# The delta output's gating in two parts: scaling two chunks ahead and transposing one chunk ahead of the product, in one raw tile each, with the first two chunks scaled in the attention half

## The chip, the cores and the metric

The kernel runs on one core of one Trainium2 chip. The metric is device time in microseconds (us), the median of the runs; lower is better. The engines are TensorE (PE, matmuls and transposes; PEld is its weight load), VectorE (DVE), ScalarE (ACT), GpSimd (POOL), and SyncE (SP), which here only issues DMAs. Each takes its instructions in the order of its own queue.

## The reference

One encoder layer in float32 over 1024 tokens of width 1024: a windowed attention (8 heads of 64) and a gated delta rule in both directions (4 heads of 128) read the same projection. Their outputs stand side by side and go through one output matrix. Then comes a feed-forward part (FFN) of width 4096.

```python
xn = _rmsnorm(h, norm_mix_w[l])
proj = xn @ w_in[l]
...
o_fwd = _chunk_gated_delta_rule(q, k, v, g[:, :, 0], beta[:, :, 0])
o_bwd = flip(_chunk_gated_delta_rule(flip(q), flip(k), flip(v), flip(g[:, :, 1]), flip(beta[:, :, 1])))
o = _rmsnorm(o_fwd + o_bwd, norm_w) * jax.nn.silu(z.astype(f32).reshape(B, S, GDN_HEADS, GDN_HEAD_DIM))
...
h = h + jnp.concatenate([attn, gdn], axis=-1) @ w_out[l]
hn = _rmsnorm(h, norm_ffn_w[l])
h = h + jnp.square(jax.nn.relu(hn @ w_ffn_in[l])) @ w_ffn_out[l]
```

The lines that matter here are `o`, the "delta output": per token and head it is divided by its root mean square, multiplied by a weight and by the gate silu(z), and multiplied with the lower half of `w_out`.

## The kernel before

Tokens are worked on in eight chunks of 128, numbered 7 down to 0 in the output stage. Each float32 product is made of three products of rounded parts: every operand is split into a high part (a cast on ACT, `split`, L123) and a low part (the difference, POOL, L124). `mm3` (L136 to L138) issues high by high, high by low, low by high.

The stage around the change is two streams woven together by `weave`. One is the output: `attention`, then `out_attn` (the attention half of the output product, chunks 7 to 0, two halves of 12 matmuls each with the output's columns), then `columns` (the operands of the first FFN column group, from the first FFN weights), then `out_all` (the delta half). The other is the delta rule's two scans. `scan` (L789) goes over the chunks one after the other; each step is a chain of small PE products (L820) and DVE steps (L833, L838, L839, L848, L859, L866). The backward scan goes from chunk 7 to 0, adds its part to the output `o` of the chunk (L866), and enters the chunk in `self.scanned`.

`out_gdn` (L915) prepares one chunk of the delta half:

- the load of silu(z) from DRAM to `zc[:, 0]` (SP, L919);
- four squares with their sums (ACT, L924), four small steps (DVE, L926 to L929), a power (POOL, L930);
- the scaling of `o` into `zc[:, 1]` (DVE, L931);
- four transposes (PE, L935), held behind the last product issued by `issue_after(self.summing)`;
- the gating by weight and silu(z) into `mix` (DVE, L936);
- cast and split into `mh` and `ml` (ACT L123, POOL L124), the operands of the chunk's product.

`out_all` (L941) calls it for up to three chunks in advance while they are scanned, and then issues the product (`out_gemm`, L892). That adds each half to the chunk's row `h` (DVE, L900). The row is stored (L953) and normalised for the FFN (ACT L213, POOL L200 and L201, DVE L215). From the fifth chunk on, the transposes of normalised rows for the FFN (`tokens_second`, PE L219) are woven in.

Buffers come from pools of fixed number by tag. Raw tiles (`wr`) have 4 buffers: the attention half's loaded rows, the first FFN weights (two, held until late in the stage), and `mix` and `zc` of each delta chunk. `pt` has 12, PSUM has 4 for `psA` and 4 for `psB`. A load waits on SP until its buffer is free, and SP's queue waits with it.

The order on each engine is not the order of the code: a scheduler fixes it when the program is built, from its own estimate of times, with the code's order as priority. So a change of the code may also exchange instructions elsewhere.

Of the kernel before, what the change touches and what calls it, by code (L numbers as in the profile page):

```python
# [17 lines left out]
P = 128  # L18
SEQ = 1024
D = 1024  # L20
NT = SEQ // P
NK = D // P
HALF = 512
GH = 4
# [54 lines left out]
class Block:  # L79
# [823 lines left out]
    def out_attn(self):  # L903

        while len(self.wo[0]) < 4:
            yield 0.5
        for c in range(NT - 1, -1, -1):
            mix = self.wr((P, 4, P))
            self.nc.sync.dma_start(out=mix, in_=self.mad[c].rearrange("p (g q) -> p g q", g=4))
            mh, ml = self.pt((P, 4, P), F32R), self.pt((P, 4, P), F32R)  # L910
            self.split(mix, mh, ml)
            self.h[c] = self.load_x(c)
            yield from self.out_gemm(self.h[c], mh, ml, self.wo[0])

    def out_gdn(self, c):  # L915

        nc = self.nc
        mix, zc = self.wr((P, GH, P)), self.wr((P, 2, GH, P))
        nc.sync.dma_start(out=zc[:, 0], in_=self.zd[:, :, c * P:(c + 1) * P].rearrange("h p t -> p h t"))  # L919
        o = self.o[c // 2][:, c % 2]  # L920
        so, f = self.small((P, GH)), self.small((P, GH))
        scr = self.small((P, P), bufs=2, tag="scr")
        for h in range(GH):
            nc.scalar.activation(out=scr, in_=o[:, h, :], func=AF.Square, accum_out=so[:, h:h + 1])  # L924
        s2 = self.sq2[:, :, c]
        nc.vector.tensor_tensor(out=so, in0=so, in1=s2, op=ALU.mult)  # L926
        nc.vector.tensor_scalar(out=so, in0=so, scalar1=1.0 / P, scalar2=EPS, op0=ALU.mult, op1=ALU.add)
        nc.vector.reciprocal(out=so, in_=so)
        nc.vector.tensor_tensor(out=so, in0=so, in1=s2, op=ALU.mult)  # L929
        nc.gpsimd.tensor_tensor(out=f, in0=so, in1=self.half_exp[:, 0:4], op=ALU.pow)  # L930
        nc.vector.tensor_tensor(out=zc[:, 1], in0=o, in1=f.unsqueeze(2).to_broadcast([P, GH, P]), op=ALU.mult)  # L931
        ps = self.ps("psA", (P, GH, P))
        with self.tc.issue_after(self.summing):
            for h in range(GH):
                nc.tensor.transpose(ps[:, h, :], zc[:, 1, h, :], self.ident)  # L935
        nc.vector.scalar_tensor_tensor(out=mix, in0=ps, scalar=self.w_gdn, in1=zc[:, 0], op0=ALU.mult, op1=ALU.mult)  # L936
        mh, ml = self.pt((P, GH, P), F32R), self.pt((P, GH, P), F32R)
        self.split(mix, mh, ml)
        return mh, ml

    def out_all(self, chunks):  # L941
        while len(self.wo[1]) < 4:
            yield 0.5
        ready, coming = [], list(chunks)
        for c in chunks:
            while c not in self.scanned:
                yield 0.5
            while coming and coming[0] in self.scanned and len(ready) < (3 if coming[0] else 2):
                ready.append(self.out_gdn(coming.pop(0)))
            if self.summed:  # L950
                self.norm_h(self.summed[-1])
            yield from self.out_gemm(self.h[c], *ready.pop(0), self.wo[1])
            self.nc.sync.dma_start(out=self.hd[c], in_=self.h[c])  # L953
            self.summed.append(c)

# [340 lines left out]
    def phases(self):  # L1296
# [11 lines left out]
        for half in range(2):  # L1308
# [5 lines left out]
            else:  # L1314
# [12 lines left out]
        self.kc, self.qc = [None] * 4, [None] * 4  # L1327
        self.qs = []
        self.wo, self.hnt, self.scanned, self.summed, self.rows = [{}, {}], [None, None], set(), [], {}
        run(weave((chain(self.proj_conv(C_GV, "v"), self.proj_z(), self.proj_attn()), 145.0),  # L1330
                  (chain(self.prep(), self.eliminate(), self.diag_blocks(), self.invert(tt, (0, 1))), 100.0)))
        self.bias_table()
# [91 lines left out]
```

## Time and profile before

| what | value |
|---|---|
| median of 3 runs | 1226.01 us (1224.49 to 1228.44) |
| the profiled execution | 1226.09 us |
| its span in the profile | 1224.0 us |
| mean granted PE clock | 0.989 |
| PE busy from 450 to 500 us | 49.64 of 50 us |
| PE busy from 500 to 550 us | 47.21 of 50 us |
| PE busy from 550 to 600 us | 46.48 of 50 us |
| PE busy from 600 to 650 us | 47.17 of 50 us |
| PE busy from 700 to 800 us | 99.97 of 100 us |

A row of the timeline gives the start, the duration, the engine, the source line, the operation, output and inputs by name, and in brackets the idle time before it with what ended it. A row of a line's or tile's view gives the count and the shortest, median and longest duration in ns. A row of the table of stretches gives the length and then the busy time of each engine with the count of its instructions; PEclk is the clock that PE was granted, as a share of full speed. Matmuls overlap: one of 128x512 shows about 390 ns, but the next starts 0.23 us later. The attention half of the output product lies at about 457 to 513 us, the delta half at about 513 to 588.

### The profile page before, as it was taken

The numbers are of one execution on the slowest core, as the hardware profiler recorded it, in microseconds if no ns is written. First come the engines' busy times: TensorE is split into PE (matmuls) and PEld (weight loads), VectorE is DVE, ScalarE is ACT, GpSimd is POOL, SyncE is SP. The second block draws the span as 40 slices with busy tenths as digits, with TensorE's granted clock in tenths as the row PEclk, the third lists the DMA queues.
The fourth block names the chain that finished last, engine by engine and source line by source line (L and its number), as shares of the span: only waits on it lengthen the run. The fifth ranks groups of instructions, "written<-read, shape, count | busy, mean of one in ns | idle before, by whom it ended". The sixth has DMA issues, their size and how long they took to land. (4 is left out here: it accounts for less than half of the span.)

```text
span 1224.0 us, 18445 instructions
## 1 busy us (share of the span) xinstructions
PE 1173.7 (96%) x6482; PEld 961.9 (79%) x6482; DVE 855.7 (70%) x1482; ACT 610.4 (50%) x1331; POOL 560.2 (46%) x470
## 2 busy tenths in 40 slices
PE   6999999899889999998999999999999999999997
PEld 5788878687768878887788888888878888888885
DVE  4676667993489996675855454453698796987976
ACT  6455688425376662124755454554555444344443
POOL 5354312224321233232764453635456565565695
PEclk9999999899989999999999999999999999999999
DMA  6134344433645577222144444344789534343323
GB/s 244 52 103 145 92 170 152 162 123 113 207 146 182 157 249 269 76 95 100 56 154 157 146 154 164 130 155 146 240 275 317 200 103 163 131 159 116 103 86 138
DMA packets 121629, 187.62 MB, mean 153 GB/s; under 512 B 11043, under 2 KB 64416, under 8 KB 121537
## 3 DMA queue, kind: packets, MB, share of 16 engines
q1 hardware_dynamic: 103876, 155.20, 38.4%
q10 hardware_dynamic: 17661, 31.24, 6.8%
q8 instruction: 51, 0.84, 0.3%
q14 instruction: 41, 0.34, 0.1%
HBM read 122.39 MB, written 63.49 MB: 152 GB/s over the span
## 5 line engine op out<-in xcount | busy, mean ns | idle before, releaser
L136 PE MATMUL psA<-pg,wh 128*128 128x512 f32 x416 | 165.0, 397 | 2.1 <-ACT pt L473 2.1
L138 PE MATMUL psA<-pg,wl 128*128 128x512 f32 x416 | 164.5, 395 | 0.0
L137 PE MATMUL psA<-pg,wh 128*128 128x512 f32 x416 | 164.2, 395 | 0.0
L124 POOL TENSOR_TENSOR wl<-wr,wh 128x512 fp32r<-128x512 f32 x44 | 66.8, 1540 | 156.5 <-ACT wh L123 128.7
L1194 DVE TENSOR_TENSOR pg<-pg 128x512 fp32r<-128x512 f32 x112 | 124.3, 1145 | 12.9 <-ACT pg L1193 12.9
L124 POOL TENSOR_TENSOR wh<-wr,wh 128x512 fp32r<-128x512 f32 x32 | 47.0, 1487 | 138.2 <-ACT wh L123 138.2
L1111 ACT ACTIVATE pt<-pt 128x512 f32<-128x512 f32 x64 | 40.3, 632 | 122.6 <-DVE pt L1101 122.6
L136 PE MATMUL psA<-pg,pg 128*128 128x512 f32 x256 | 98.7, 391 | 0.9 <-DVE pg L1239 0.9
L137 PE MATMUL psA<-pg,pg 128*128 128x512 f32 x256 | 99.2, 391 | 0.1
L138 PE MATMUL psA<-pg,pg 128*128 128x512 f32 x256 | 99.2, 389 | 0.0
L136 PEld LDWEIGHTS psA<-pg,wh 128*128 128x128 f32 x416 | 78.8, 190 | 19.5 <-ACT pt L473 2.4
L137 PEld LDWEIGHTS psA<-pg,wh 128*128 128x128 f32 x416 | 78.7, 189 | 17.9 <-issue 0.9
L138 PEld LDWEIGHTS psA<-pg,wl 128*128 128x128 f32 x416 | 78.7, 189 | 16.7
L124 POOL TENSOR_TENSOR pg<-wr,pg 128x512 fp32r<-128x512 f32 x48 | 73.2, 1559 | 37.9 <-ACT pg L123 37.9
L1193 ACT CAST pg<-pg 128x512 fp32r<-128x512 f32 x112 | 66.7, 620 | 36.4 <-DMA pg<-sd 31.3
L137 PE MATMUL psB<-pg,pg 128*128 128x512 f32 x192 | 74.9, 390 | 0.8 <-POOL pg L124 0.7
L136 PE MATMUL psB<-pg,pg 128*128 128x512 f32 x192 | 74.7, 389 | 0.0
L138 PE MATMUL psB<-pg,pg 128*128 128x512 f32 x192 | 74.7, 389 | 0.0
L123 ACT CAST wh<-wr 128x512 fp32r<-128x512 f32 x76 | 43.6, 623 | 52.1 <-PE psA L137 31.9
L1101 DVE TENSOR_TENSOR pt<-psB,pt 128x512 f32<-128x512 f32 x39 | 26.9, 690 | 57.6 <-PE psB L138 40.7
L1101 DVE TENSOR_TENSOR pt<-psA,pt 128x512 f32<-128x512 f32 x39 | 26.7, 689 | 51.3 <-PE psA L138 34.1
L136 PEld LDWEIGHTS psA<-pg,pg 128*128 128x128 f32 x256 | 48.0, 188 | 12.1 <-DVE pg L1239 2.1
(395 smaller groups left out, 3234.8 us busy)
## 6 DMA issues: line engine op xcount, KB each, us to landing
sd<-pt ACTq DMA_DIRECT2D x112, 256.0 KB, 2.1
pg<-sd SPq DMA_DIRECT2D x112, 256.0 KB, 2.9
wr<-in_w_ffn_in SPq DMA_DIRECT2D x32, 512.0 KB, 3.6
wr<-in_w_in SPq DMA_DIRECT2D x22, 512.0 KB, 4.2
pg<-in_x SPq DMA_DIRECT2D x16, 512.0 KB, 5.0
wr<-in_w_ffn_out SPq DMA_DIRECT2D x16, 512.0 KB, 4.7
sc<-kvd SPq DMA_DIRECT2D x14, 512.0 KB, 3.7
kvd<-pt SPq DMA_DIRECT2D x16, 256.0 KB, 2.4
```

The lines of the kernel that those rows point to most:

```text
L123: a = nc.scalar.copy(out=h, in_=raw)
L124: b = (eng or nc.gpsimd).tensor_tensor(out=l, in0=raw, in1=h.bitcast(F32), op=ALU.subtract)
L136: nc.tensor.matmul(ps, wh, xh, start=first, stop=False, skip_group_check=onto)
L137: nc.tensor.matmul(ps, wh, xl, start=False, stop=False, skip_group_check=onto)
L138: return nc.tensor.matmul(ps, wl, xh, start=False, stop=last, skip_group_check=onto)
L1101: self.nc.vector.tensor_tensor(out=out, in0=in0, in1=in1, op=ALU.add)
L1111: self.nc.scalar.activation(out=c, in_=c, func=AF.Relu)
L1193: nc.scalar.copy(out=s[:, 0], in_=raw)
L1194: v.tensor_tensor(out=s[:, 1], in0=raw, in1=s[:, 0].bitcast(F32), op=ALU.subtract)
```

## The change

`out_gdn` is cut into two. `out_scaled` does everything up to the scaling and returns the chunk and its raw tile. `out_gated` does the transposes, the gating and the split. The gated result is written over the scaled tile `zc[:, 1]`, and the tile `mix` is gone.

In the attention half, chunk 7 is scaled after attention chunk 2's product, chunk 7 is gated after chunk 1's, and chunk 6 is scaled after chunk 0's. In the delta half, before the product of chunk c, all chunks down to c−2 are scaled (waiting, in the generator, for the scan to have passed them) and all down to c−1 are gated.

```diff
             yield from self.out_gemm(self.h[c], mh, ml, self.wo[0])
-
-    def out_gdn(self, c):
-
-        nc = self.nc
-        mix, zc = self.wr((P, GH, P)), self.wr((P, 2, GH, P))
+            if c in (2, 0):
+                while self.coming[0] not in self.scanned:
+                    yield 0.5
+                self.scaled.append(self.out_scaled(self.coming.pop(0)))
+            if c == 1:
+                self.ready.append(self.out_gated(*self.scaled.pop(0)))
+
+    def out_scaled(self, c):
+
+        nc = self.nc
+        zc = self.wr((P, 2, GH, P))
...
         nc.vector.tensor_tensor(out=zc[:, 1], in0=o, in1=f.unsqueeze(2).to_broadcast([P, GH, P]), op=ALU.mult)
+        return c, zc
+
+    def out_gated(self, c, zc):
+
+        nc = self.nc
+        mix = zc[:, 1]
         ps = self.ps("psA", (P, GH, P))
...
-        ready, coming = [], list(chunks)
         for c in chunks:
-            while c not in self.scanned:
-                yield 0.5
-            while coming and coming[0] in self.scanned and len(ready) < (3 if coming[0] else 2):
-                ready.append(self.out_gdn(coming.pop(0)))
+            while self.coming and c - self.coming[0] < 3:
+                while self.coming[0] not in self.scanned:
+                    yield 0.5
+                self.scaled.append(self.out_scaled(self.coming.pop(0)))
+            while self.scaled and c - self.scaled[0][0] < 2:
+                self.ready.append(self.out_gated(*self.scaled.pop(0)))
...
-            yield from self.out_gemm(self.h[c], *ready.pop(0), self.wo[1])
+            yield from self.out_gemm(self.h[c], *self.ready.pop(0), self.wo[1])
```

In the changed kernel the lines are numbered anew: the load of z is L925, the squares L930, the small steps L932 to L935, the power L936, the scaling L937, the transposes L947, the gating L948, and the first FFN sums L1086 and L1088 (before L1073 and L1075).

Three places show how the queues change. The first is PE's queue where the attention half ends. Before, `psA_5527` is attention chunk 0's product, and `psA_5578` and `psA_5604` are the transposes of delta chunks 7 and 6; the `psB` rows are scan products.

```order
L138 MATMUL psA_5527<-wh_4792,pt_5508 128x512
L935 MATMUL psA_5578<-ident,wr_5563 128x128 x4
L820 MATMUL psB_5227<-sc_5066,pg_3943 128x128 x2
L820 MATMUL psB_5232<-sc_5162,pt_5164 128x128 x2
L820 MATMUL psB_5255<-sc_5162,pg_3942 128x128 x2
L820 MATMUL psB_5260<-sc_5162,pg_3942 128x128 x2
L935 MATMUL psA_5604<-ident,wr_5589 128x128 x4
L820 MATMUL psB_5265<-sc_5250,pg_2578 128x128 x2
```

In the changed kernel `psA_5506` is attention chunk 1's product, `psA_5520` the transposes of delta chunk 7, and `psA_5538` and `psA_5552` the two halves of attention chunk 0's product.

```order
L138 MATMUL psA_5506<-wh_4792,pt_5469 128x512
L947 MATMUL psA_5520<-ident,wr_5451 128x128 x4
L820 MATMUL psB_5208<-sc_5162,sc_5161 128x128 x2
L820 MATMUL psB_5213<-sc_5162,sc_5161 128x128 x2
L820 MATMUL psB_5218<-sc_5066,pg_3943 128x128 x2
L820 MATMUL psB_5223<-sc_5162,pt_5164 128x128 x2
L820 MATMUL psB_5227<-sc_5066,pg_3943 128x128 x2
L820 MATMUL psB_5232<-sc_5162,pt_5164 128x128 x2
L136 MATMUL psA_5538<-pg_4677,pt_5532 128x512
L137 MATMUL psA_5538<-pg_4678,pt_5532 128x512
L136 MATMUL psA_5552<-pg_4677,pt_5532 128x512
L137 MATMUL psA_5552<-pg_4678,pt_5532 128x512
```

Chunk 7's transposes moved ahead of attention chunk 0's product, and that product now stands between scan products.

The second place is PE's queue at delta chunk 1's transposes. Before, `psA_5840` is chunk 4's product, `psA_5871` are chunk 1's transposes, and `psA_5888` is chunk 3's product; no scan product is left.

```order
L138 MATMUL psA_5840<-pg_4971,pt_5691 128x512
L935 MATMUL psA_5871<-ident,wr_5856 128x128 x4
L136 MATMUL psA_5888<-pg_5155,pt_5753 128x512
L137 MATMUL psA_5888<-pg_5156,pt_5753 128x512
L138 MATMUL psA_5888<-pg_5155,pt_5754 128x512
```

In the changed kernel `psA_5885` is chunk 3's product, `psA_5915` are chunk 1's transposes, and `psA_5933` is chunk 2's product.

```order
L820 MATMUL psB_5493<-sc_5429,pt_5431 128x128 x2
L820 MATMUL psB_5497<-sc_5340,pg_3716 128x128 x2
L820 MATMUL psB_5502<-sc_5429,pt_5431 128x128 x2
L137 MATMUL psA_5885<-pg_4971,pt_5799 128x512
L138 MATMUL psA_5885<-pg_4970,pt_5800 128x512
L947 MATMUL psA_5915<-ident,wr_5839 128x128 x4
L136 MATMUL psA_5933<-pg_5155,pt_5860 128x512
L137 MATMUL psA_5933<-pg_5156,pt_5860 128x512
```

Chunk 1's transposes moved one product later, and the scan's last products now lie within chunk 3's product.

The third place is DVE's queue at the first FFN sums, which read both first FFN weight tiles. Before, they stand where attention chunk 3's additions (`pg_5281`) are.

```order
L900 TENSOR_TENSOR pg_5281<-pg_5281,psA_5325 128x512
L1073 SCALAR_TENSOR_TENSOR pt_5545<-wr_5541,wr_5543 128x512
L848 SCALAR_TENSOR_TENSOR sc_5066<-sc_4977,egl,psB_5112 128x128 x2
L1075 TENSOR_TENSOR wr_5541<-wr_5541 128x4x128
L848 SCALAR_TENSOR_TENSOR sc_5066<-sc_4977,egl,psB_5117 128x128 x2
```

In the changed kernel `pg_5536` is attention chunk 0's row, and `wr_5602` is delta chunk 5's raw tile.

```order
L833 SCALAR_TENSOR_TENSOR sc_5250<-psB_5255,negc,sc_5250 128x128 x2
L937 TENSOR_TENSOR wr_5602<-dbl_4251,sm_5605 128x512
L833 SCALAR_TENSOR_TENSOR sc_5250<-psB_5260,negc,sc_5250 128x128 x2
L1086 SCALAR_TENSOR_TENSOR pt_5585<-wr_5581,wr_5583 128x512
L1088 TENSOR_TENSOR wr_5581<-wr_5581 128x4x128
L900 TENSOR_TENSOR pg_5536<-pg_5536,psA_5538 128x512
L838 TENSOR_TENSOR sc_5251<-psB_5265,w_533 128x256
L839 TENSOR_TENSOR sc_5251<-psB_5265,cc 128x256
```

The sums moved three chunks later, between two steps of the scan. On SP the load of the second weight tile (L254) now stands behind the z loads of chunks 7 and 6 and takes its raw buffer from chunk 7.

More of the change, by code (lines that the diff above doesn't have):

```diff
@@ L1329, in phases @@
         self.wo, self.hnt, self.scanned, self.summed, self.rows = [{}, {}], [None, None], set(), [], {}
+        self.scaled, self.ready, self.coming = [], [], list(range(NT - 1, -1, -1))
         run(weave((chain(self.proj_conv(C_GV, "v"), self.proj_z(), self.proj_attn()), 145.0),
```

## The prediction

> **What bounds the kernel now.** I read the page first, then the table of stretches, then the waits, and the timeline of the stretch where TensorE (PE) waits.
>
> ```profile
> span 1224.0 us, 18445 instructions
> PE 1173.7 (96%) x6482; PEld 961.9 (79%) x6482; DVE 855.7 (70%) x1482; ACT 610.4 (50%) x1331; POOL 560.2 (46%) x470
> ```
>
> PE is busy for 96% of the span and no other engine comes near. A change can therefore save time only where PE idles or runs slowly. It touches the output product, near 450 to 600 us.
>
> ```profile
> core 0: us, PE busy (x) PEld busy (x) DVE busy (x) ACT busy (x) POOL busy (x), PEclk, DMA share, GB/s
> 502.66:513.00 10.34, 10.34 (x59) 9.03 (x58) 5.46 (x14) 0.86 (x2) 0.16 (x1) 1.00 0.01 2
> 513.00:524.00 11.00, 8.21 (x61) 7.05 (x60) 10.27 (x23) 2.66 (x5) 8.11 (x6) 1.00 0.28 95
> 524.00:550.00 26.00, 26.00 (x157) 22.87 (x156) 19.35 (x55) 6.97 (x23) 7.98 (x10) 1.00 0.29 101
> 556.00:560.00 4.00, 1.26 (x7) 0.84 (x6) 1.75 (x5) 0.00 (x0) 1.01 (x1) 0.86 0.32 131
> 560.00:563.00 3.00, 3.00 (x10) 2.41 (x9) 0.75 (x1) 1.67 (x3) 1.08 (x1) 0.62 0.13 39
> ...
> 606.00:620.00 14.00, 14.00 (x64) 11.58 (x63) 6.94 (x10) 10.24 (x20) 14.00 (x11) 1.00 0.29 95
> ```
>
> From 502.66 to 513 and from 524 to 550 PE never stops. It loses time from 513 to 524, where DVE is full (10.27 of 11.00 us), and around 558. From 560 to 563 it is busy but at a granted clock of 0.62. From 606 on it is full again. The PE timeline names what it waited for; these are all its idle pieces between 513 and 574.5:
>
> ```profile
> 517.19 0.66 PE L935 MATMUL psA<-ident,wr 128*128 128x128 f32 x4 [1.27 <-DVE wr L931]
> ...
> 519.50 0.71 PE L820 MATMUL psB<-sc,sc 128*128 128x128 f32 x4 [0.45 <-DVE sc L838]
> 520.81 0.71 PE L820 MATMUL psB<-sc,sc 128*128 128x128 f32 x4 [0.61 <-DVE sc L838]
> ...
> 523.43 0.66 PE L935 MATMUL psA<-ident,wr 128*128 128x128 f32 x4 [0.46 <-DVE wr L931]
> ...
> 550.41 0.66 PE L935 MATMUL psA<-ident,wr 128*128 128x128 f32 x4 [0.27 <-DVE wr L931]
> ...
> 559.28 1.11 PE L935 MATMUL psA<-ident,wr 128*128 128x128 f32 x4 [2.74 <-DVE wr L931]
> ...
> 574.15 0.66 PE L935 MATMUL psA<-ident,wr 128*128 128x128 f32 x4 [0.51 <-DVE wr L931]
> ```
>
> Five of the seven are transposes (L935) of a scaled delta chunk that wait for its scaling (L931). They stand in PE's queue ahead of products that were ready, so these wait too. The other two are scan products (L820) waiting for VectorE (DVE). The sum is 1.27+0.45+0.61+0.46+0.27+2.74+0.51 = 6.31 us.
>
> **The change, part by part.** Number and kind of instructions stay the same: eight scalings, eight times four transposes, eight gatings and splits. Only the order changes, and one raw tile for each chunk goes. So the sum is made of waits and of clock.
>
> *Waits that go.* In the new PE queue chunk 7's transposes stand behind attention chunk 1's second product, and chunk c−1's stand behind chunk c's product. Is the scaled tile there by then? I put PE's new order on the clock by its own pitches:
>
> ```profile
> 502.66 0.39 PE L136 MATMUL psA<-pg,pt 128*128 128x512 f32 x1
> ...
> 552.98 0.39 PE L136 MATMUL psA<-pg,pt 128*128 128x512 f32 x1
> ...
> 555.93 0.39 PE L137 MATMUL psA<-pg,pt 128*128 128x512 f32 x1
> ...
> 509.01 1.05 PE L820 MATMUL psB<-sc,sc 128*128 128x128 f32 x8
> ...
> 510.71 0.48 PE L136 MATMUL psA<-pg,pt 128*128 128x512 f32 x1
> ...
> 530.77 0.60 PE L935 MATMUL psA<-ident,wr 128*128 128x128 f32 x4
> 531.12 0.48 PE L136 MATMUL psA<-pg,pt 128*128 128x512 f32 x1
> ```
>
> Thirteen products start in 2.95 us, 0.227 us each. A scan row of two heads takes 0.445 us: four take 509.01 to 510.71, plus 0.08 because the first product after them has a pitch of 0.31. Four transposes cost 0.43 us in the same way. Between attention chunk 1's product (502.66 in the trace) and chunk 0's transposes (574.15) both queues hold 192 products, 36 scan rows, seven sets of transposes of delta chunks and three of token rows: 43.7 + 16.0 + 3.0 + 1.3 = 64.0 us. The trace needs 71.5 us. So 7.5 us lie here: 6.31 of waits, and 1.2 of slow clock. The clock checks this: 3.00 us at 0.62 lose 1.14, and the first transposes of 559.28 some more.
>
> In the new order, started at 502.66 without waits, the transposes of chunks 7, 6, 5, 4, 3, 2, 1 and 0 fall at about 509.0, 519.4, 527.0, 535.7, 543.4, 551.1, 559.6 and 566.8. The chain before a transpose has these durations:
>
> ```profile
> L924 ACT ACTIVATE scr<-dbl x32: 293/310/312, 452.0 to 570.6; 128x128 f32<-128x128 f32 x32
> L924 ACT ACTIVATION_READ_ACCUMULATOR scr<-dbl x32: 185/186/194, 452.3 to 570.8; 128x1 f32 x32
> L929 DVE TENSOR_TENSOR sm<-sm,sq x8: 154/166/742, 457.5 to 571.7; 128x4 f32<-128x4 f32 x8
> L930 POOL TENSOR_TENSOR sm<-sm,half_exp x8: 1007/1012/1029, 459.4 to 572.0; 128x4 f32<-128x4 f32 x8
> L931 DVE TENSOR_TENSOR wr<-dbl,sm x8: 677/692/1623, 486.0 to 573.4; 128x512 f32<-128x512 f32 x8
> ```
>
> Four squares with their read-outs (0.31 and 0.19, a little overlapped: 1.7), four small DVE steps like L929 (0.8 with their gaps), the power 1.0, the scaling 0.7, and about 0.8 of handing over make 5.0 us; with DVE's queue around them I get 5.7. Chunks 7 to 4 are scanned by 499, chunk 4 last:
>
> ```profile
> 498.55 0.42 DVE L866 TENSOR_TENSOR dbl<-dbl,psB 128x256 f32<-128x256 f32 x1 [0.53 <-PE psB L820]
> ```
>  Chunks 3, 2, 1 and 0 get their last scan sum at about 513, 531, 547 and 560, and so lie 30, 20, 12 and 6.8 us ahead of their transposes. The tightest is chunk 0, with about 1 us to spare. So none of the five waits should stay. The two scan waits go too: in that stretch PE now has attention chunk 0's product, 24 × 0.227 = 5.5 us, between the scan's steps.
>
> *Behind the transposes* come gating (L936), cast and split:
>
> ```profile
> L936 DVE SCALAR_TENSOR_TENSOR wr<-psA,cols,wr x8: 732/744/751, 514.3 to 575.3; 128x512 f32<-128x512 f32 x8
> L123 ACT CAST pt<-wr x8: 617/620/622, 515.1 to 576.1; 128x512 fp32r<-128x512 f32 x8
> L124 POOL TENSOR_TENSOR pt<-wr,pt x8: 1283/1293/1728, 516.5 to 576.8; 128x512 fp32r<-128x512 f32 x8
> ```
>
> In sum 0.74 + 0.62 + 1.29 and hand-overs, about 3.5 us from the transposes' start to the split's end. The next chunk's product follows, except for chunk 7, only after the current product's remaining work or a whole product of 5.5 us. Chunk 7 needs its operand at 519.8 and has it at 512.5; chunk 6 has it at 524 and needs it at 528. One raw buffer less for each chunk frees the buffers earlier. Each load of z then waits only for the split two chunks earlier and has 3 us or more until its gating. I cost all this at nothing; the product of the current chunk hides it, and without it each chunk would cost up to 3.5 us.
>
> *Waits that come.* First, attention chunk 0's cast and split now stand behind chunk 7's on ScalarE and POOL. By the durations above its low half is ready at about 513.8, and PE asks for it at 513.9. A split of 1.73 in place of 1.28 us makes up to 0.9 us of wait. Second, the second half of the first FFN weights needs the raw buffer that chunk 7's split returns at 512.5. Its load
>
> ```profile
> wr<-in_w_ffn_in SPq DMA_DIRECT2D x32, 512.0 KB, 3.6
> ```
>
> lands at about 516.5. Before, the first two of these sums took
>
> ```profile
> 491.69 1.20 DVE L1073 SCALAR_TENSOR_TENSOR pt<-wr,wr 128x512 f32<-128x512 f32 x1
> ...
> 493.33 0.68 DVE L1075 TENSOR_TENSOR wr<-wr 128x512 f32<-128x512 f32 x1
> ```
>
> and now DVE's first FFN sum (L1073, new L1086) stands in order behind scan step L833 and waits for it. Queued behind are the sum's second step, two output additions (L900) and the scan's L838 and L839. DVE needs 1.20 + 0.68 for the sums and some 1.3 for an addition and the two scan rows, 3.2 us, so it is ready at about 519.9, and PE wants it at 523.2: 3.3 us to spare. On SP the z loads of chunks 5 and 4 and the scan's last but one key load stand behind this weight load; that key load now issues near 515, and before at
>
> ```profile
> 515.58 0.46 SPq L813 DMA_DIRECT2D sc<-kvd  x1
> ```
>
> At least nothing is lost; at most 0.9 us at the first place and 2.0 at the second (below). I take 0.4 us, near the lower end, since both places come out just covered.
>
> [...] The scaling has two operands in SBUF, and its rows spread from 0.68 to 1.62 us. The slowest ran while POOL was at two splits:
>
> ```profile
> 515.51 1.62 DVE L931 TENSOR_TENSOR wr<-dbl,sm 128x512 f32<-128x512 f32 x1
> ```
>
> ```profile
> 514.08 2.51 POOL L124 TENSOR_TENSOR wh<-wr,wh 128x512 fp32r<-128x512 f32 x2
> ```
>  [...]
>
> [...]
>
> [...] The row has 0.62 after a gap of 2.74 us. [...]
>
> *Elsewhere.* Three places in the first FFN groups have products exchanged. PE is full there (606 to 620) and their operands are split well before, so I cost them at nothing; at worst one product set of 12 × 0.227 = 2.7 us waits.
>
> **The sum.** 6.31 + 1.2 − 0.4 = 7.1 us. The profiled execution took 1226.09 us, 2.09 more than its span and 0.08 above the median of 1226.01. So 1226.09 − 7.1 = 1219.0 us, 0.58% less. The stage of token transposes behind it moves as a whole, because it starts from PE.
>
> **Rivals.**
> *The wait moves to DVE* (0.13). [...] For it: DVE is full from 513 to 524. Against: the spare times above.
> *The scan is the limit* (0.11). If the scan's alternation of PE and DVE sets the end, earlier gating buys only the 2.74 gap or less, given back at the next wait: 1223.5 to 1226.5. For it: two of the seven waits are scan's. Against: from 524 to 550 scan and products shared PE without a gap. That the order does not do what it says is not open, since the rows show the transposes moved.
> *Slower: the last chunk's chain holds PE* (0.06). Chunk 0's squares stood behind a normalisation on ScalarE:
>
> ```profile
> 550.98 0.42 DVE L866 TENSOR_TENSOR dbl<-dbl,psB 128x256 f32<-128x256 f32 x1
> ...
> 568.70 0.29 ACT L924 ACTIVATE scr<-dbl 128x128 f32<-128x128 f32 x1
> ```
>
> From its last scan sum to its transposes (574.15) passed 22.8 us. Between them now lie 6.8 us of PE work. Beyond that each us costs one. At the old length it is 16 us lost against 7.5 won, some 1234; from 14.3 us of chain on the kernel is slower than before. Against: in the new ScalarE queue those squares stand ahead of that normalisation.
>
> **How the numbers follow.** Forecast 0.70 (1217 to 1221), the rivals 0.13, 0.11, 0.06. About 0.3% (3.7 us) is what a measurement can tell from no change, so the line lies at 1222.3. Faster by more: forecast plus part of the first rival, 0.79. Within: the rest of the first and the second, 0.15. Slower: 0.06. The range reaches from 1216.5 (0.5 below the forecast's low end, for a token stage that gains too) to 1223.5, the first rival's end.
>
> **What would show it.** No wait above 0.3 us before transposes (now L947) or scan products from 513 to 570; a granted clock of 1.00 there; chunk 0's transposes 7 us earlier, near 567; DVE's first FFN sum starting near 517. A wait at products of attention chunk 0 near 514, or before scan rows near 523, would be the first rival; one before the last transposes the third. I would be wrong if gaps come back after 570 in the token stage or in the FFN groups.

## The result, and the profile after

| kernel | median | runs |
|---|---|---|
| before | 1227.15 us (1224.49 to 1232.53) | 10 |
| changed | 1218.57 us (1217.60 to 1222.88) | 10 |

The ratio is 0.9934, with a 95% interval of 0.9923 to 0.9946, so the changed kernel is faster by 0.54 to 0.77%. Its profiled execution took 1218.1 us. The forecast was 1219.0, with a range of 1216.5 to 1223.5.

The page of the changed kernel, its first lines:

```profile
span 1216.4 us, 18458 instructions
...
PE 1172.0 (96%) x6482; PEld 960.5 (79%) x6482; DVE 855.4 (70%) x1482; ACT 610.8 (50%) x1331; POOL 559.8 (46%) x470
```

The span is 7.6 us shorter, and PE was busy 1.7 us less (1173.7 before) for the same 6482 instructions: 5.9 us of idle time went, and some slow matmuls. The table of stretches of the changed kernel shows where:

```profile
core 0: us, PE busy (x) PEld busy (x) DVE busy (x) ACT busy (x) POOL busy (x), PEclk, DMA share, GB/s
513.00:524.00 11.00, 11.00 (x62) 9.51 (x61) 9.09 (x19) 3.01 (x5) 6.56 (x5) 1.00 0.36 113
...
556.00:560.00 4.00, 4.00 (x28) 3.54 (x27) 2.81 (x7) 1.61 (x8) 0.00 (x0) 1.00 0.00 1
560.00:563.00 3.00, 3.00 (x17) 2.49 (x16) 1.55 (x6) 2.24 (x4) 1.99 (x2) 1.00 0.43 175
...
597.30:601.30 4.00, 3.99 (x11) 3.14 (x12) 2.99 (x5) 4.00 (x9) 4.00 (x5) 0.57 0.00 0
```

From 513 to 524 PE is busy for all 11.00 us (8.21 before), from 556 to 560 for all 4.00 (1.26), and from 560 to 563 its clock is 1.00 (0.62). The last row is new: right behind the token stage PE is busy at a clock of 0.57, where the kernel before ran at 1.00 (its row stands further down, with the second profiles). PE's timeline of the changed kernel, with the transposes of chunks 7, 1 and 0, and then the idle pieces of the token stage:

```profile
507.68 0.60 PE L947 MATMUL psA<-ident,wr 128*128 128x128 f32 x4
...
558.60 0.60 PE L947 MATMUL psA<-ident,wr 128*128 128x128 f32 x4
...
565.87 0.60 PE L947 MATMUL psA<-ident,wr 128*128 128x128 f32 x4
...
593.95 0.63 PE L219 MATMUL psB<-ident,sc 128*128 128x128 f32 x4 [0.73 <-DVE pt L1045]
...
595.93 0.63 PE L219 MATMUL psB<-ident,sc 128*128 128x128 f32 x4 [1.35 <-DVE pt L1045]
...
597.31 0.65 PE L136 MATMUL psB<-pg,wh 128*128 128x512 f32 x1 [0.76 <-DVE pt L1054]
597.76 0.63 PE L137 MATMUL psB<-pg,wh 128*128 128x512 f32 x1
```

No row of L947 has a bracket: none of the transposes waits. The three pieces of the token stage (0.73, 1.35, 0.76) are those of before, moved as a whole. But the matmuls behind them now take 0.63 us in place of 0.39, and start some 0.43 us apart (597.31 to 597.76) in place of 0.227.

Where the 7.6 us lie is read from four rows that both queues hold. First the kernel before, then the changed one; they are a scan product that waits for L839, the first product behind the token stage (597.31 in the rows above), the first product at which PE waits in the last FFN groups, and one behind it. The second row of each fence is the start of attention chunk 1's product, needed further down:

```profile
445.67 0.68 PE L820 MATMUL psB<-sc,pt 128*128 128x128 f32 x4 [0.55 <-DVE sc L839]
...
499.94 0.39 PE L136 MATMUL psA<-pg,pt 128*128 128x512 f32 x1
...
605.61 0.47 PE L136 MATMUL psB<-pg,wh 128*128 128x512 f32 x1 [0.76 <-DVE pt L1041]
...
906.50 0.50 PE L136 MATMUL psB<-dbl,sc 128*128 128x512 f32 x1 [2.08 <-ACT pt L1106]
...
991.95 0.50 PE L136 MATMUL psA<-pg,pg 128*128 128x512 f32 x1 [0.29 <-DVE pg L1239]
```

```profile
446.22 0.68 PE L820 MATMUL psB<-sc,pt 128*128 128x128 f32 x4 [0.55 <-DVE sc L839]
...
501.31 0.39 PE L136 MATMUL psA<-pg,pt 128*128 128x512 f32 x1
...
899.93 0.50 PE L136 MATMUL psB<-dbl,sc 128*128 128x512 f32 x1 [1.53 <-ACT pt L1119]
...
983.75 0.50 PE L136 MATMUL psA<-pg,pg 128*128 128x512 f32 x1 [0.29 <-DVE pg L1252]
```

| stretch | before | changed | difference |
|---|---|---|---|
| start to the scan product | 445.67 | 446.22 | +0.55 |
| to behind the token stage | 159.94 | 151.09 | −8.85 |
| to the FFN product near 900 | 300.89 | 302.62 | +1.73 |
| to the one behind it | 85.45 | 83.82 | −1.63 |
| to the end | 232.05 | 232.65 | +0.60 |

The stage that the change touches gained 8.85 us in these two executions (8.2 in the second profiles, 158.56 and 150.34, where neither had a slow clock within the stage). Behind it 1.73 were given back and 1.63 gained again, and neither was forecast. The experiments ask what in the change made the 8.85, and what the other two are.

### The profile page after: what moved, and what is told of

It reads as the page before. It is cut to its first block, busy times and chain, and to the rows that moved or that the text cites. A ratio compares the mean times of both kernels' runs of the same rounds, so it can differ in the third digit from the quotient of the medians.

```text
span 1216.4 us, 18458 instructions
## 1 busy us (share of the span) xinstructions
PE 1172.0 (96%) x6482; PEld 960.5 (79%) x6482; DVE 855.4 (70%) x1482; ACT 610.8 (50%) x1331; POOL 559.8 (46%) x470
```

## The experiments

Each kernel was timed in several rounds beside the kernel before on the same chip, except the second profile of the kernel before. "Pieces" are PE's idle pieces in the timeline from 505 to 576 us, nearly all ahead of transposes and scan products, 6.31 us in sum before and none in the changed kernel.

The first theory was that of the prediction: the gain comes from where the transposes stand in PE's queue. Its rivals were that the freed buffer, the attention part or the earlier scaling is what pays.

**The buffer alone.**

```diff
-        mix, zc = self.wr((P, GH, P)), self.wr((P, 2, GH, P))
+        zc = self.wr((P, 2, GH, P))
+        mix = zc[:, 1]
```

> The kernel before, with the gated product written into the scaled half of its raw tile, so that one raw buffer less is held for each chunk; the order stays as it was. Theory (the gain comes from where the transposes stand in PE's queue): the buffer alone is worth nothing, 0.998 to 1.001 of the time before, and idle pieces of some 1 us ahead of the first transposes and of 2 to 3 us ahead of chunk 1's transposes stay. Rival (the buffer that comes free earlier is what pays, by earlier loads): 0.993 to 0.996, and the piece ahead of chunk 1's transposes shrinks below 1 us.

Measured: 0.9983 (0.9971 to 0.9995). The pieces at chunks 2, 1 and 0 came out as before (0.27, 2.74, 0.51). Those from 513 to 524 shrank from 2.79 to one of 1.10, where the scheduler placed the first transposes otherwise. The kernel gained 0.17% (0.05 to 0.29) of the 0.66%; that it comes from this other order is likely and not shown. The waits at the later transposes did not get shorter. The opposite, two raw tiles with the look-ahead of two, wasn't tried.

**Without the attention part.**

```diff
             yield from self.out_gemm(self.h[c], mh, ml, self.wo[0])
-            if c in (2, 0):
...
-            if c == 1:
-                self.ready.append(self.out_gated(*self.scaled.pop(0)))
```

> The changed kernel without its attention part: chunks 7 and 6 are scaled and gated only when the second half of the output product starts; from there on scaling is two chunks and gating one chunk ahead. Theory: the pieces from 545 us on (0.27, 2.74 and 0.51 us idle and the slow clock, some 5.6 us from start to start in the trace before) go, those from 514 to 524 us (some 3.7 us from start to start) stay at least by half: 0.9945 to 0.9965. Rival (the attention part carries the gain, the rest only keeps it): above 0.997. Rival (the attention part is not needed): 0.9925 to 0.994.

Measured: 0.9946 (0.9933 to 0.9959), and no piece at all. The pieces from 513 to 524 went too, which was not expected: only two sets of transposes stand ahead of the first delta product here, and that product lies between the scan's products. The attention part is not needed for the pieces; on time the two kernels' intervals overlap.

**The attention part alone**, `out_all` as before:

```diff
-            while self.coming and c - self.coming[0] < 3:
...
+            while self.coming and self.coming[0] in self.scanned and len(self.ready) < (3 if self.coming[0] else 2):
+                self.ready.append(self.out_gated(*self.out_scaled(self.coming.pop(0))))
```

> The attention part of the change alone: chunk 7 is scaled and gated and chunk 6 scaled within the attention half, but from then on up to three gated chunks are kept ready as in the kernel before, each gated as soon as it is scaled, so that a chunk's transposes stand ahead of the product two chunks before it. Theory: the 3.7 us near 514 to 524 go, but PE then reaches the later transposes sooner and waits there for the scan's last sums and the scaling, at least 3 us idle in sum ahead of the transposes of chunks 2, 1 and 0: 0.996 to 0.9985. Rival (the attention part alone makes the gain): 0.9925 to 0.994 and no idle piece above 0.5 us there.

Measured: 0.9963 (0.9950 to 0.9975). From 513 to 524 PE is full; 0.22 and 0.22 us stand near 535, 1.80 at chunk 1 and 0.51 at chunk 0, 2.75 in sum. As the theory had it, nearly.

**Both look-aheads one chunk longer**, so that the transposes stand where they stood before:

```diff
-            while self.coming and c - self.coming[0] < 3:
+            while self.coming and c - self.coming[0] < 4:
...
-            while self.scaled and c - self.scaled[0][0] < 2:
+            while self.scaled and c - self.scaled[0][0] < 3:
```

> The changed kernel with both look-aheads one chunk longer in the second half: scaling three chunks ahead, gating (transposes) two chunks ahead, as the transposes stood before the change. Theory (the place of the transposes pays): PE meets transposes whose chunk is not scanned or scaled yet, idle pieces of 2 us or more come back ahead of chunk 1's or chunk 0's transposes: 0.996 to 0.9995. Rival (early scaling pays, wherever the transposes stand): 0.9925 to 0.9945, with no such piece.

Measured: 0.9954 (0.9939 to 0.9969), between the two. One piece is left. From the timelines of DVE and PE of this kernel, chunk 0's last scan sum and its transposes:

```profile
557.10 0.42 DVE L866 TENSOR_TENSOR dbl<-dbl,psB 128x256 f32<-128x256 f32 x1
```

```profile
561.68 0.65 PE L947 MATMUL psA<-ident,wr 128*128 128x128 f32 x4 [3.28 <-DVE wr L937]
```

They come 4.2 us behind the sum's end, which is the bare chain: here PE is simply too early for the scan. But at chunk 1, with its transposes at the old place, the 2.74 us are gone. That speaks against the place as the cause there. The next two kernels move the place without scaling earlier.

**One number in the kernel before**, two gated chunks kept ready instead of three:

```diff
-            while coming and coming[0] in self.scanned and len(ready) < (3 if coming[0] else 2):
+            while coming and coming[0] in self.scanned and len(ready) < 2:
```

> The kernel before with one number changed: at most two gated chunks are kept ready in place of three, so that a chunk's transposes stand one product later in PE's queue. No scaling ahead, no attention part, the separate raw tile stays. Theory (the gain comes from the place of the transposes alone): the pieces ahead of the transposes after 545 us go, 0.9935 to 0.9955, as without the attention part (0.9946). Rival (a place later needs the scaling in two parts, since scaling right beside the transposes comes late): idle pieces of 1 us or more stay ahead of transposes after 525 us, 0.9965 or more.

Measured: 0.9985 (0.9977 to 0.9994), against the theory. The pieces are 1.27 near 519, 0.22 and 0.22 near 537, and 1.74, 1.67 and 0.92 at chunks 2, 1 and 0, 6.04 in sum.

**Scaling and gating in one part again**, one chunk ahead, chunk 7 in the attention half:

```diff
...
-            while self.coming and c - self.coming[0] < 3:
+            while self.coming and c - self.coming[0] < 2:
                 while self.coming[0] not in self.scanned:
                     yield 0.5
-                self.scaled.append(self.out_scaled(self.coming.pop(0)))
-            while self.scaled and c - self.scaled[0][0] < 2:
-                self.ready.append(self.out_gated(*self.scaled.pop(0)))
+                self.ready.append(self.out_gated(*self.out_scaled(self.coming.pop(0))))
```

> The changed kernel with scaling and gating in one part again, one chunk ahead of its product, and chunk 7 still within the attention half. Theory (place alone): as the changed kernel, 0.9925 to 0.9945, and no idle piece above 0.3 us ahead of transposes from 505 to 570 us. Rival (the earlier scaling pays): pieces of 0.3 to 1.5 us at several transposes, 0.995 to 0.998.

Measured: 1.0001 (0.9993 to 1.0010). With the transposes a product later and one raw tile the whole gain is gone, and the theory of the place falls. PE's timeline of this kernel, chunks 2, 1 and 0:

```profile
555.90 0.66 PE L945 MATMUL psA<-ident,wr 128*128 128x128 f32 x4 [1.74 <-DVE wr L935]
...
563.69 0.66 PE L945 MATMUL psA<-ident,wr 128*128 128x128 f32 x4 [1.67 <-DVE wr L935]
...
573.57 1.11 PE L945 MATMUL psA<-ident,wr 128*128 128x128 f32 x4 [2.38 <-DVE wr L935]
```

The transposes follow each other by 7.8 and 9.9 us, though chunk 1 was scanned by 545.40 and chunk 0 by 553.47 (the ends of their last L866). Something ties one set to the next. The rows of ACT, POOL and DVE between the transposes of chunk 2 and chunk 1 show it:

```profile
557.38 0.62 ACT L123 CAST pt<-wr 128x512 fp32r<-128x512 f32 x1 [5.70 <-DVE wr L946]
557.90 1.05 ACT L213 ACTIVATE pt<-pg 128x1024 bf16<-128x1024 f32 x1
...
558.95 0.30 ACT L928 ACTIVATE scr<-dbl 128x128 f32<-128x128 f32 x1
```

```profile
561.90 1.01 POOL L934 TENSOR_TENSOR sm<-sm,half_exp 128x4 f32<-128x4 f32 x1 [1.62 <-DVE sm L933]
```

```profile
562.94 0.69 DVE L935 TENSOR_TENSOR wr<-dbl,sm 128x512 f32<-128x512 f32 x1 [0.20 <-POOL sm L934]
```

Chunk 1's squares (558.95) stand in ACT's queue behind chunk 2's cast (557.38), and the cast waits for chunk 2's gating, that is for chunk 2's transposes. So a **ring** runs from one set of transposes to the next: transposes, gating, cast, normalisation, squares, small steps, power, scaling, transposes. It takes 7.8 us or more, while PE has a product and a set of transposes, some 6 us. The kernel before has the same ring at its largest piece. Its rows of ACT, and of DVE with chunk 1's last scan sum ahead of its scaling:

```profile
552.15 0.62 ACT L123 CAST pt<-wr 128x512 fp32r<-128x512 f32 x1 [6.64 <-DVE wr L936]
552.68 1.05 ACT L213 ACTIVATE pt<-pg 128x1024 bf16<-128x1024 f32 x1
...
553.73 0.29 ACT L924 ACTIVATE scr<-dbl 128x128 f32<-128x128 f32 x1
```

```profile
542.07 0.41 DVE L866 TENSOR_TENSOR dbl<-dbl,psB 128x256 f32<-128x256 f32 x1
...
558.54 0.69 DVE L931 TENSOR_TENSOR wr<-dbl,sm 128x512 f32<-128x512 f32 x1 [1.19 <-POOL sm L930]
```

Chunk 1 was scanned at 542.48, but its squares began at 553.73, 11.2 us later. Ahead of them ACT idled for 6.64 us at a cast that waited for chunk 2's gating. From transposes to transposes (550.41 to 559.28) it is 8.87 us. In the changed kernel ACT's rows stand the other way round:

```profile
547.39 0.31 ACT L930 ACTIVATE scr<-dbl 128x128 f32<-128x128 f32 x1 [1.01 <-DVE dbl L866]
...
551.58 0.62 ACT L123 CAST pt<-wr 128x512 fp32r<-128x512 f32 x1 [3.34 <-DVE wr L948]
...
557.95 0.31 ACT L930 ACTIVATE scr<-dbl 128x128 f32<-128x128 f32 x1 [4.71 <-DVE dbl L866]
...
560.31 0.62 ACT L123 CAST pt<-wr 128x512 fp32r<-128x512 f32 x1 [0.36 <-DVE wr L948]
```

The third of chunk 1's squares (547.39) stands ahead of chunk 2's cast at 551.58, and chunk 0's first (557.95) ahead of chunk 1's cast at 560.31. What both wait for is the scan (L866). The ring is the new theory, and four kernels test it.

**The squares alone one chunk earlier**, in the kernel with one part:

```diff
+            for n in range(max(c - 2, 0), c):
+                while n not in self.scanned:
+                    yield 0.5
+                if n not in self.squared:
+                    self.out_squared(n)
             while self.coming and c - self.coming[0] < 2:
-                while self.coming[0] not in self.scanned:
-                    yield 0.5
...
```

> The one-part kernel (scaling and gating one chunk ahead, chunk 7 in the attention half; 1.0001 of the time before) with one thing moved: the four squares of a chunk on ScalarE are issued one chunk earlier; the small steps, the power and the scaling stay beside the gating. New theory, the ring on ScalarE: a chunk's squares stood in ScalarE's queue behind the cast of the chunk before it, which waits for that chunk's transposes, so from one set of transposes to the next runs a chain of 7.8 to 9.9 us (transposes, gating, cast, squares, small steps, power, scaling) where PE has only some 6 us of work. With the squares out of it the chain is some 6.6 us (gating 0.96, cast 0.8, split 1.35, POOL's two small steps 0.8, power 1.0, scaling 0.9, transposes and hand-overs 0.8): the pieces of 1.74, 1.67 and 2.38 us fall below 0.8 each, 0.994 to 0.997. Rival (the scaling on VectorE has to be early, the squares don't matter): pieces of 1.5 us or more stay, 0.999 or more.

Measured: 0.9937 (0.9919 to 0.9955), from 1.0001 to the time of the changed kernel by writing four instructions for each chunk earlier. The transposes of chunks 2, 1 and 0 in PE's timeline have no bracket left:

```profile
550.18 0.60 PE L953 MATMUL psA<-ident,wr 128*128 128x128 f32 x4
557.47 0.60 PE L953 MATMUL psA<-ident,wr 128*128 128x128 f32 x4
564.75 0.60 PE L953 MATMUL psA<-ident,wr 128*128 128x128 f32 x4
```

The only piece from 505 to 576 is 0.26 us at attention chunk 0's product. The scaling on DVE didn't have to be written earlier. The fall is larger than expected. The edit does one thing more: like the changed kernel, it waits in the generator until chunk c−2 is scanned before chunk c's product is written, and PE's queue came out otherwise as well (8 scan products in a row ahead of chunk 3's transposes in place of 28). That wait was not tried alone. But between the transposes of chunks 1 and 0 PE has the same work in both kernels, 24 product matmuls and 12 token transposes: 9.88 us in the one-part kernel (563.69 to 573.57), 7.28 here (557.47 to 564.75).

**The squares held behind the cast**, in the changed kernel:

```diff
-        for h in range(GH):
-            nc.scalar.activation(out=scr, in_=o[:, h, :], func=AF.Square, accum_out=so[:, h:h + 1])
+        with self.behind(self.cast):
+            for h in range(GH):
+                nc.scalar.activation(out=scr, in_=o[:, h, :], func=AF.Square, accum_out=so[:, h:h + 1])
...
-        self.split(mix, mh, ml)
+        self.cast = self.split(mix, mh, ml)[:1]
...
+            while self.scaled and c - self.scaled[0][0] < 2:
+                self.ready.append(self.out_gated(*self.scaled.pop(0)))
             while self.coming and c - self.coming[0] < 3:
...
-            while self.scaled and c - self.scaled[0][0] < 2:
-                self.ready.append(self.out_gated(*self.scaled.pop(0)))
```

> The changed kernel with scaling written behind gating and the squares of a chunk held in ScalarE's queue behind the cast of the chunk gated before it; transposes, look-ahead of two and one, one raw tile and the attention part stay. Ring theory: the chain from transposes to transposes closes again, some 7.5 us (without the 1.05 us of the normalisation that also stood in it), and pieces of 0.7 to 2 us come back ahead of the transposes of chunks 3 to 0: 0.996 to 0.9995. Rival (what counts is that scaling is issued two chunks ahead, whatever stands ahead of it on ScalarE): 0.9925 to 0.995 and no piece above 0.5 us.

Measured: 0.9952 (0.9937 to 0.9967). Two pieces came back, 0.91 at chunk 5 and 1.38 at chunk 1:

```profile
527.64 0.66 PE L948 MATMUL psA<-ident,wr 128*128 128x128 f32 x4 [0.91 <-DVE wr L938]
...
560.26 0.66 PE L948 MATMUL psA<-ident,wr 128*128 128x128 f32 x4 [1.38 <-DVE wr L938]
```

The direction is the ring's, the size is smaller than expected, and on time alone the kernel is not told from the changed one. The normalisation (1.05 us) stood behind the squares here and not in the ring, and ahead of the transposes of chunks 4, 3, 2 and 0 PE had scan or token products to do, which can have covered the rest; that was not tried apart.

**Scaling early alone**, the kernel without the attention part with the longer look-aheads:

```diff
-            while self.coming and c - self.coming[0] < 3:
+            while self.coming and c - self.coming[0] < 4:
...
-            while self.scaled and c - self.scaled[0][0] < 2:
+            while self.scaled and c - self.scaled[0][0] < 3:
```

> The kernel without the attention part, scaling three and gating two chunks ahead: scaling early, but the transposes where they stood before the change. With the kernels before it this fills a table of four: neither (1), transposes later alone (0.9985), both (0.9946), and this one, scaling early alone. Ring theory: the squares of chunk 1 no longer stand behind chunk 2's cast and the 2.74 us piece goes, but the transposes of chunks 7, 6 and 5 again stand in a row ahead of the first product, with 1 to 2 us of idle pieces from 513 to 524, and those of chunk 0 ahead of its scan and scaling, some 3 us: 0.996 to 0.9985. Rival (early scaling is the whole gain): 0.994 to 0.9955.

Measured: 0.9946 (0.9929 to 0.9962), the rival's figure. The pieces are 1.18 near 520 and 0.30 at chunk 0 (no 3 us there), 1.48 in sum. So with the squares ahead of the cast the transposes may stand where they stood before the change and most of the gain stays, though with the attention part chunk 0's then waited 3.28 us.

**The smallest edit on the kernel before**, the squares alone ahead:

```diff
...
+            for n in range(max(c - 3, 0), c):
+                if n in coming and n in self.scanned and n not in self.squared:
+                    self.squared[n] = self.out_squared(n)
             while coming and coming[0] in self.scanned and len(ready) < (3 if coming[0] else 2):
```

> The kernel before with only the squares of a chunk issued up to three chunks ahead of its product, where it is scanned by then, and so ahead of the cast of the chunk gated before it; small steps, power, scaling, transposes and gating in one part, three gated chunks kept ready, two raw tiles, no attention part. Ring theory: the 2.74 us piece ahead of chunk 1's transposes falls below 1 us and the 0.51 ahead of chunk 0's goes; from 510 to 525 us the transposes of chunks 7, 6 and 5 still stand in a row ahead of the first delta product, with 1 to 3 us of idle pieces: 0.994 to 0.9975. Rival (the transposes must stand later, or scaling in two parts, as well): 0.998 or more, with pieces of 1.5 us or more ahead of chunk 1's or chunk 0's transposes.

Measured: 0.9990 (0.9976 to 1.0004), less than the ring theory had, and not told from no change. PE's timeline of this kernel, all its pieces:

```profile
520.78 0.71 PE L820 MATMUL psB<-sc,pg 128*128 128x128 f32 x4 [0.37 <-DVE sc L848]
...
523.53 0.66 PE L942 MATMUL psA<-ident,wr 128*128 128x128 f32 x4 [1.00 <-DVE wr L938]
...
525.24 0.75 PE L820 MATMUL psB<-sc,pg 128*128 128x128 f32 x4 [0.48 <-DVE sc L833]
...
526.75 0.75 PE L820 MATMUL psB<-sc,pg 128*128 128x128 f32 x4 [0.76 <-DVE sc L833]
...
529.03 0.66 PE L942 MATMUL psA<-ident,wr 128*128 128x128 f32 x4 [0.98 <-DVE wr L938]
...
559.38 0.66 PE L942 MATMUL psA<-ident,wr 128*128 128x128 f32 x4 [0.57 <-DVE wr L938]
```

At chunk 1 0.57 is left of 2.74, and at chunk 0 nothing: there the ring is undone. But from 520 to 529 it is 3.59 us, more than the 2.79 of before. So there is a second cause, at the first place: three sets of transposes stand ahead of the first delta product with nothing but scan products between, and PE waits for DVE in turn with each. The ring doesn't make these, and the squares don't cure them; the change does. Which part of it does is not shown: the kernel with two ready has only two sets there and keeps 1.27, scaling early alone has three and keeps 1.18, and nothing above 0.3 us from 513 to 524 is left only with fewer sets and early squares together, or with the attention part.

**Both kernels a second time**, for the clock.

> The changed kernel, not altered, profiled and timed a second time. In its first profile matmuls ran at 0.63 us in place of 0.39 for 3.4 us behind the token stage's idle pieces (0.73, 1.35 and 0.76 us near 596), where the kernel before had the same pieces and no slow matmuls; and none behind 1.53 us near 900, where the kernel before had slow ones behind 2.08. Theory A (a slow stretch follows from the idle pieces alone): both come out again as they were. Theory B (it is a matter of the phase in which the pieces fall, so the places differ between profiles of one program): at least one of the two places comes out otherwise, and the span differs by about 1.6 us for each. The time: 0.9925 to 0.9945 by both.

> The kernel before, not altered, profiled a second time. Theory A: slow matmuls again behind the 2.74 us piece near 559 and the 2.08 us piece near 906, none behind the token stage's pieces near 604. Theory B: at least one of these three comes out otherwise. By both the seven idle pieces from 513 to 574 us come out again within 0.2 us each, 6.0 to 6.6 us in sum.

Measured: the changed kernel 0.9941 (0.9928 to 0.9954). The seven pieces of the kernel before came out again to 0.01 us each, 6.31 in sum. The clock did not. The tables of stretches, first of the two profiles of the kernel before, behind the 2.74 us piece and behind the token stage, then of the changed kernel's second profile:

```profile
559.00:563.00 4.00, 3.71 (x12) 3.13 (x13) 0.98 (x2) 1.67 (x3) 1.08 (x1) 0.59 0.19 65
605.50:610.50 5.00, 4.89 (x22) 4.09 (x23) 3.99 (x6) 5.00 (x11) 5.00 (x5) 1.00 0.00 0
```

```profile
561.50:565.50 4.00, 3.57 (x18) 3.03 (x19) 1.13 (x2) 1.67 (x3) 1.30 (x2) 1.00 0.32 108
606.50:610.50 4.00, 3.66 (x16) 3.09 (x17) 2.99 (x6) 4.00 (x9) 4.00 (x4) 1.00 0.00 0
```

```profile
597.00:601.00 4.00, 4.00 (x11) 3.14 (x12) 2.99 (x5) 4.00 (x9) 4.00 (x5) 0.57 0.00 0
```

The same 2.74 us were followed by a clock of 0.59 in one profile and of 1.00 in the other. From the scan product to behind the token stage the second one took 158.56 us against 159.94, so the slow clock was worth 1.38. The changed kernel had slow matmuls behind the token stage again and none near 900 again, and the kernel before had them near 900 again. So the 2.74 us piece came out otherwise, as theory B has it, and the other places repeated. That it is the phase that decides is not shown.

The kernels together:

| kernel | squares behind the cast | sets of transposes ahead of the first delta product | pieces | ratio |
|---|---|---|---|---|
| before | yes | 3 | 6.31 | 1 |
| one raw tile | yes | 3 | 4.62 | 0.9983 |
| one number: two ready | yes | 2 | 6.04 | 0.9985 |
| one part | yes | 2, one in the attention half | 6.51 | 1.0001 |
| attention part alone | yes | 3, one in the attention half | 2.75 | 0.9963 |
| squares held behind the cast | yes | 2, one in the attention half | 2.29 | 0.9952 |
| squares alone, from before | no | 3 | 4.16 | 0.9990 |
| scaling early alone | no | 3 | 1.48 | 0.9946 |
| both look-aheads longer | no | 3, one in the attention half | 3.28 | 0.9954 |
| no attention part | no | 2 | 0 | 0.9946 |
| squares early, one part | no | 2, one in the attention half | 0.26 | 0.9937 |
| changed | no | 2, one in the attention half | 0 | 0.9934 |

No kernel beat the changed one. The pieces alone don't give the ratios: a slow stretch behind the token stage or near 900, up to some 1.6 us each, stands in some of these profiles and not in others.

## Why the prediction came out as it did

*The time* was right: 1219.0 forecast, 1218.57 measured, inside the range; by the medians the gain is 8.6 us, where 7.1 was forecast. *The waits that go* went, all seven. The transposes fell at 507.68 to 565.87 where the prediction had 509.0 to 566.8, in part by luck: the prediction let the work start 2.7 us late (see the sum of the stage, below), and in the changed kernel it started 1.4 us later than before.

*The reason given for five of them* was wrong in part. The prediction said that transposes stand ahead of products that were ready, and that a product more between them covers the chain from the last scan sum. Its chain of 5.0 us was the right size (4.2 bare, with the transposes two ahead), but it let it start at the scan. It started at the cast of the chunk before, as the rows of ACT at 552 show. That is shown for the largest, chunk 1's; at chunk 0 the squares stood behind a normalisation that ACT began at 567.65 after 4.75 us idle, and the first two (1.27 and 0.46) lie at the place with the second cause. A later place without the squares ahead leaves 6.04 or 6.51 us of pieces. The prediction had the row that shows it: the third rival named chunk 0's squares behind a normalisation, but didn't ask what that normalisation and the cast ahead of it waited for, nor saw the same at chunk 1.

*The two scan waits* went for about the reason given, that products now lie between the scan's steps; that this doesn't need the attention part was not foreseen.

*The sum of the stage* was too small, 7.1 against 8.85. The step that failed is the stretch from 502.66. That row is the second half of attention chunk 1's product; the product starts at 499.94, so the kernel before spent 74.2 us on 64.0 us of work and lost 10.2, not 7.5. (The changed kernel spends 64.56 from 501.31 to 565.87, 9.65 less. Ahead of these rows it took 0.8 us more in this execution, 55.09 from 446.22 against 54.27 from 445.67, and not in its second one, 54.34 from 446.64 to 500.98, so the change does not explain it.) The 6.31 us of pieces hid the error: a bracket counts from the end of the last matmul, and matmuls that start every 0.227 us take 0.39. From the product at 555.93 to the transposes at 559.28 it is 3.35 us, where two pitches take 0.45: 2.90 lost under a bracket of 2.74. In the second profiles, without a slow clock there, the same rows lie 72.72 us apart in the kernel before (502.66 to 575.38) and 64.57 in the changed one (500.98 to 565.55): 8.15 us, with 6.31 in brackets, so 1.8 us stand in none. The term of waits was thus 8.15 in place of 6.31, and the slow clock 1.5 (74.21 − 72.72) in place of 1.2.

*The clock* was mis-sized as a term of the kernel. The 1.2 us were there in that execution (1.38 by the second profile), and not in the next. What was missed is the token stage: its pieces stayed, and in the changed kernel slow matmuls follow them, some 8 that start 0.2 us later each, 1.6 us. That is the +1.73 of the third row of the table, less what else changed there.

*The new waits* (0.4) did not come. Attention chunk 0's product had no wait near 512, and the scan rows near 523 none: the first rival, a wait of PE on DVE, found nothing at its two places. In the kernel with early squares 0.26 us came at the first of them. On DVE a late weight load and a long scaling are there, but smaller than the time to spare:

```profile
515.21 0.69 DVE L1086 SCALAR_TENSOR_TENSOR pt<-wr,wr 128x512 f32<-128x512 f32 x1 [1.05 <-DMA wr<-in_w_ffn_in]
...
523.22 1.54 DVE L937 TENSOR_TENSOR wr<-dbl,sm 128x512 f32<-128x512 f32 x1
```

The sum waited 1.05 us for its weight load and yet started at 515.21, ahead of the 517 forecast. No run shows the 2.0 us that the prediction allowed as the most at the second place, from which it took its 0.4: of DVE's steps there one scaling took 0.85 us more (1.54 in place of 0.69), and the four FFN sums took 0.69 each. That scaling began while POOL was at a split (522.94 to 524.20). In the first profiles of both kernels the four scalings that began during a split took 1.24 to 1.75 us, and the other twelve 0.68 or 0.69.

*Elsewhere* was put at nothing. Near 900 the piece fell from 2.08 to 1.53 us and the slow clock behind it went, −1.63 us in the next stretch. Near there, DVE steps took 0.68 or 1.7 us; of the last three ahead of this product (L1162 to L1164, new L1175 to L1177) two were long before (0.86, 1.68 and 1.76 us) and one after (1.18, 1.67 and 0.68). That this comes from the change is not shown: the kernel without the attention part has 2.22 there and the one-part kernel 1.64.

So the total is right partly since errors cancel: 1.75 us too little in the stage, against 1.73 given back behind it.

*The rivals.* That the scan is the limit was true for one kernel, the transposes two ahead (3.28 us for chunk 0). The slower case didn't arise; the one-part kernel shows how it would have looked, a ring that holds PE at chunks 2, 1 and 0, and even that cost no more than before.

## What to carry to other kernels

When PE waits for a chain over other engines, follow the chain back to where it started late, not to where its data were ready: here the squares' data lay ready for 11.2 us, and for 6.6 of them ACT stood at a cast that waited for PE itself. Here such a ring through in-order queues was undone by moving its earliest instruction ahead of the waiting one; moving the consumer later only shifted the ring. That need not be the whole gain: from the kernel before, the squares alone shortened the ring's piece from 2.74 to 0.57 us and the time by 0.1%, which is not told from none, as waits of another kind stayed ahead of it. And take the price of an idle piece from start to start against the pitch, over a stretch whose ends are the same rows in both queues.

## What the runs showed of the hardware

The slow clock hangs on more than the length of one piece. Near 900 us, seven of fourteen profiles had a piece of 2.03 to 2.92 us and all had slow matmuls behind it (in the kernel before seven of 0.63 us in place of 0.39, from 907.10 on); the other seven had 1.47 to 1.67 and none had. But 2.74 us near 560 came with and without, and the token stage's three pieces, 2.5 to 3.0 us in sum within 4 us, had slow matmuls behind them in nine profiles and not in five. The longest slow stretches last about 3.4 us (597.31 to 600.75 in the changed kernel), with a start every 0.43 us in place of 0.227; others have 5 to 7 such matmuls in place of 8.

Why the token stage is hit in the changed kernel each time and in the kernel before neither time stays open.
